# A hybrid decoder trunk on eight cores: the S5 scan and the dilated attention written in large operations, and TensorE's waits on its own semaphore left out

## The chip, the cores and the metric

The kernel runs on the eight cores of one Trainium2 chip. Each core runs the same program over one whole sequence of 8192 tokens (core c takes sequence c mod 4), in 32 tiles of 256 tokens. The metric is the device time of the slowest core in microseconds (us). The engines have their profile names here: PE is TensorE (matmuls) and PEld its weight loads, DVE is VectorE, ACT is ScalarE, POOL is GpSimd, and SP issues the DMAs. SBUF is the memory on the core from which the engines read, PSUM the banks into which matmuls sum, and an evacuation copies a bank to SBUF. In some executions the cores of one die (cores 0 to 3, or 4 to 7) show a lower granted clock and take longer; a run with one die over 1% longer than the other counts as slow.

## The reference

Two layers. Layer 0 has an SSD mixer and an S5 mixer side by side; layer 1 has causal attention in three patterns of (window, dilation), merged by their denominators. After each mixer comes a gated FFN. Norms, conditioning and the SSD mixer are left out here, because the change does not touch them.

```python
D_MODEL, BATCH, SEQ = 1024, 4, 8192
S5_N_GROUPS, S5_STATE = 64, 64                       # 4096 complex states
ATT_PATTERNS = ((128, 1), (512, 4), (2048, 16))      # (window, dilation); 8 heads of 128
FFN_HIDDEN = 2816

def complex_linear_combine(e1, e2):                  # h(t) = a * h(t-1) + b(t), complex
    a1r, a1i, b1r, b1i = e1
    a2r, a2i, b2r, b2i = e2
    return (a2r * a1r - a2i * a1i, a2r * a1i + a2i * a1r,
            a2r * b1r - a2i * b1i + b2r, a2r * b1i + a2i * b1r + b2i)
...
    bu_re = jnp.einsum('lgc,gpc->lgp', us, bb_re)    # S5: input, scan, output
    bu_im = jnp.einsum('lgc,gpc->lgp', us, bb_im)
    _, _, h_re, h_im = lax.associative_scan(complex_linear_combine, (ar, ai, bu_re, bu_im), axis=0)
    return jnp.einsum('lgp,gcp->lgc', h_re, c_re) - jnp.einsum('lgp,gcp->lgc', h_im, c_im)
...
def dilated_window_attention(q, k, v, window, dilation):
    # query t attends t - j*dilation, j = 0..window//dilation
    ...
    p = jnp.exp(s - s_max)
    den = jnp.sum(p, axis=-1, keepdims=True)
    o = jnp.einsum('brnhqk,brnkhe->brnqhe', p / den, vb)
...
def swiglu(h, w_in, w_out):
    g, u = jnp.split(h @ w_in, 2, axis=-1)
    return (jax.nn.silu(g) * u) @ w_out
```

## The kernel before

A small scheduler in Python records every operation with the buffers that it reads and writes, and derives the waits. A buffer keeps the token (engine, count) of its last writer. The engine that comes next waits for that count, even if it is itself the writer.

```python
    def _collect(self, eng, reads, writes, extra=()):
        waits = {}
        seen = self.seen[eng]

        def add(tok):
            if tok is None:
                return
            k, v = tok
            if seen.get(k, 0) >= v:
                return
            if waits.get(k, 0) < v:
                waits[k] = v

        for b in reads:
            add(b.w)
        for b in writes:
            add(b.w)
            for t in b.r:
                add(t)
        ...
```

So eight matmuls that sum into one PSUM bank each wait for the one before. Weights stream from DRAM in panels of up to 1 MB through three slots; a projection asks for a panel when it begins with it, and one DMA queue (SP) carries all loads and stores in program order.

```python
    def wpanel(self, name, kc, c0, cols, k0=0):
        slot = self.wp_rr
        self.wp_rr = (self.wp_rr + 1) % self.NW                  # NW = 3
        ...
        s.dma(lambda e, a=view, b=src: e.dma_start(out=a, in_=b), reads=[self.w_buf[name]], writes=[self.b_wp[slot]])
...
    def ffn(self, li):
        for mp in range(0, FC, 4):                               # FC = 22: six pairs of panels
            wg, bwg = self.wpanel(win, KC, mp * 128, nm * 128)
            wu, bwu = self.wpanel(win, KC, FFN_H + mp * 128, nm * 128)
            for mi in range(nm):
                # 8 matmuls with wg into one bank, 8 with wu into another, then silu and product
...
    def mixer1(self, ti):
        self.proj("attn_w_qkv", 0, 3072, KC, hrhs, self.b_h, on_q)
        def mk_kv(dst, bdst):
            def on_kv(mi, mw, ps, bps):
                q = mi % 2
                self.evac("act" if mi % 2 == 0 else "dve", self.kvst[:, q, :], ps[:, 0:NT], [bps], [self.b_kvst[q]])
                s.dma(lambda e: e.dma_start(out=dst[mi, :, 2048 + t0:2048 + t0 + NT], in_=self.kvst[:, q, :]),
                      reads=[self.b_kvst[q]], writes=[bdst])
            return on_kv
        self.proj("attn_w_qkv", 3072, 1024, KC, hrhs, self.b_h, mk_kv(self.Kd, self.b_Kd))
        self.proj("attn_w_qkv", 4096, 1024, KC, hrhs, self.b_h, mk_kv(self.Vd, self.b_Vd))
        for h in range(8):
            self.attn_head(ti, h)
```

The S5 mixer goes through blocks of 32 tokens, eight a tile. TensorE computes the inputs, ScalarE brings them to SBUF, VectorE (one half of the states) and GpSimd (the other) step through time, and TensorE forms the outputs. Attention goes key block by key block, up to 44 a head.

The softmax here doesn't subtract the row's maximum and nothing guards it: scores larger than these inputs give would overflow.

Of the kernel before, what the change touches and what calls it, by code (L numbers as in the profile page):

```python
# [24 lines left out]
class Sched:  # L25
# [22 lines left out]
    def _collect(self, eng, reads, writes, extra=()):  # L48
        waits = {}
        seen = self.seen[eng]  # L50

        def add(tok):
            if tok is None:
                return
            k, v = tok
            if seen.get(k, 0) >= v:
                return
            if waits.get(k, 0) < v:
# [8 lines that stand above are left out]
        for t in extra:  # L67
            add(t)
        for k, v in waits.items():
            seen[k] = v  # L70
        return list(waits.items())
# [14 lines left out]
    def op(self, eng, fn, reads=(), writes=()):  # L86
        waits = self._collect(eng, reads, writes)
# [103 lines left out]
class Builder:  # L191
# [18 lines left out]
    def _tensors(self):  # L210
# [46 lines left out]
        self.ps_rr = 0  # L257

    POOL_BANKS = (0, 1, 2, 3, 7)
# [173 lines left out]
    def _tensors_mix(self):  # L433
# [37 lines left out]
        self.Hall = self.sb("Hall", [128, 2, 32, 33], F32); self.b_Hall = [s.buf("Hall0"), s.buf("Hall1")]  # L471
        self.Hs16 = self.sb("Hs16", [128, 2, 32, 32], BF16); self.b_Hs16 = s.buf("Hs16")
        self.t12 = self.sb("t12", [128, 2, 2, 2, 16], F32); self.b_t12 = [s.buf("t12a"), s.buf("t12b")]
# [7 lines left out]
        assert o <= 7424, o  # L481
        a16 = self.A16
# [43 lines left out]
    def setup_mix(self):  # L526
# [15 lines left out]
        for hf in range(2):  # L542
            s.op("pool", lambda e, hf=hf: e.memset(self.Hall[:, :, hf * 16:(hf + 1) * 16, :], 0.0), writes=[self.b_Hall[hf]])
# [7 lines left out]
    def setup_s5(self):  # L551
# [12 lines left out]
        def coeffs(lr, li, ld, N, base):  # L564
# [3 lines left out]
            act(lambda e: e.activation(out=dt, in_=ld, func=AF.Exp))  # L568
            dve(lambda e: e.tensor_tensor(mag, lr, dt, ALU.mult))
# [27 lines left out]
        dve(lambda e, ai=ai: e.tensor_scalar(self.s5c[:, 3, :], ai, -1.0, None, ALU.mult), writes=[self.b_s5w])  # L597
        N = 128
# [147 lines left out]
    def ssd_chunk(self, c, ac, dtv, dtw, bd, idf):  # L746
# [11 lines left out]
        px, bpx = self.psum()  # L758
# [9 lines left out]
        pb, bpb = self.psum()  # L768
# [58 lines left out]
    def s5_sub(self, ts, T):  # L827
        s = self.s
        for b in range(4):
            ri = b // 2  # L830
            pb, bpb = self.psum()
            for slot in range(16):
                q = (b % 2) * 16 + slot
                fc, rb = q // 4, q % 4
                s.op("pe", lambda e, pb=pb, slot=slot, fc=fc, rb=rb, ri=ri: e.matmul(  # L835
                    pb[:, slot * T:(slot + 1) * T], self.Wb[32 * rb:32 * rb + 32, fc, ri, :], self.ubf[32 * rb:32 * rb + 32, fc, ts:ts + T],
                    start=True, stop=True, tile_position=(32 * rb, 0)), reads=[self.b_s5w, self.b_ubf[fc]], writes=[bpb])
            hf = b % 2
            s.op("act", lambda e, pb=pb, ri=ri, hf=hf: e.activation(out=self.Hall[:, ri, hf * 16:(hf + 1) * 16, 1:1 + T],  # L839
                                                                  in_=pb[:, :].rearrange("p (q t) -> p q t", q=16), func=AF.Copy),  # L840
                 reads=[bpb], writes=[self.b_Hall[hf]])
        for hf, eng in ((0, "dve"), (1, "pool")):
            qs = slice(hf * 16, (hf + 1) * 16)
            t1 = self.t12[:, hf, 0, :, :]
            t2 = self.t12[:, hf, 1, :, :]
            bh = self.b_Hall[hf]
            bt = self.b_t12[hf]
            for t in range(1, T + 1):
                s.op(eng, lambda e, t=t, t1=t1, qs=qs: e.tensor_tensor(t1, self.s5c[:, 0:2, qs], self.Hall[:, :, qs, t - 1], ALU.mult),  # L849
                     reads=[bh, self.b_s5w], writes=[bt])  # L850
                s.op(eng, lambda e, t=t, t2=t2, qs=qs: e.tensor_tensor(t2[:, 0, :], self.s5c[:, 3, qs], self.Hall[:, 1, qs, t - 1], ALU.mult),  # L851
                     reads=[bh, self.b_s5w], writes=[bt])
                s.op(eng, lambda e, t=t, t2=t2, qs=qs: e.tensor_tensor(t2[:, 1, :], self.s5c[:, 2, qs], self.Hall[:, 0, qs, t - 1], ALU.mult),  # L853
                     reads=[bh, self.b_s5w], writes=[bt])
                s.op(eng, lambda e, t1=t1, t2=t2: e.tensor_tensor(t1, t1, t2, ALU.add), reads=[bt], writes=[bt])  # L855
                s.op(eng, lambda e, t=t, t1=t1, qs=qs: e.tensor_tensor(self.Hall[:, :, qs, t], self.Hall[:, :, qs, t], t1, ALU.add),  # L856
                     reads=[bt], writes=[bh])
        s.op("act", lambda e: e.activation(out=self.Hs16[:, :, :, :], in_=self.Hall[:, :, :, 1:1 + T], func=AF.Copy),  # L858
             reads=self.b_Hall, writes=[self.b_Hs16])
        for hf, eng in ((0, "dve"), (1, "pool")):  # L860
            qs = slice(hf * 16, (hf + 1) * 16)
            s.op(eng, lambda e, qs=qs: e.tensor_copy(self.Hall[:, :, qs, 0], self.Hall[:, :, qs, T]), reads=[self.b_Hs16], writes=[self.b_Hall[hf]])
        po, bpo = self.psum()
        for fc in range(8):
            n = 0
            for rb in range(4):
                q = 4 * fc + rb
                for ri in range(2):
                    s.op("pe", lambda e, fc=fc, q=q, ri=ri, n=n: e.matmul(po[:, fc * T:(fc + 1) * T], self.Wc[:, q, ri, :], self.Hs16[:, ri, q, :],  # L869
                                                                         start=(n == 0), stop=(n == 7)),  # L870
                         reads=[self.b_s5w, self.b_Hs16], writes=[bpo])
# [4 lines left out]
    def s5_tile(self):  # L876
        s = self.s
        fv = self.fvec
        T = 32
# [44 lines left out]
    def attn_block(self, qap, nq, keys, ocols, Ob, bO, Db, bD):  # L924
        s = self.s
        scale = float(128 ** -0.5)
        n = len(keys)
        for i, (kap, nk, vidx, vbuf, mask) in enumerate(keys):
            pS, bpS = self.psum()
            slot = self.pt_rr  # L930
            self.pt_rr = (self.pt_rr + 1) % 4
            pt = self.PT[0:nk, slot, 0:nq]
            bpt = self.b_PT[slot]
            s.op("pe", lambda e, pS=pS, kap=kap, nk=nk: e.matmul(pS[0:nk, 0:nq], kap, qap, start=True, stop=True),  # L934
                 reads=[self.b_Kw] + self._qbufs, writes=[bpS])
            s.op("act", lambda e, pS=pS, pt=pt, nk=nk: e.activation(out=pt, in_=pS[0:nk, 0:nq], func=AF.Exp, scale=scale),  # L936
                 reads=[bpS], writes=[bpt])
            eng = "dve" if (slot % 2 == 0) else "pool"
            s.op(eng, lambda e, pt=pt, mask=mask: e.tensor_tensor(pt, pt, mask, ALU.mult), reads=[self.b_const], writes=[bpt])  # L939
            s.op("pe", lambda e, pt=pt, i=i, nk=nk: e.matmul(Db[:, ocols], self.ones_bf[0:nk, :], pt, start=(i == 0), stop=(i == n - 1)),  # L940
                 reads=[bpt, self.b_const], writes=[bD])
            s.op("pe", lambda e, pt=pt, i=i, vidx=vidx, nk=nk: e.matmul(Ob[:, ocols], self.Vtok[0:nk, vidx, :], pt, start=(i == 0), stop=(i == n - 1)),
                 reads=[bpt, vbuf], writes=[bO])
# [200 lines left out]
```

## Time and profile before

The median was 90664.84 us over the 13 runs (90652.80 to 90679.29). A stage is cut here from its first matmul to the first matmul of the next one, on the slowest core; the medians over the tiles are:

| stage | times a tile | us each | us a tile |
|---|---|---|---|
| S5 scan | 1 | 872 | 872 |
| attention | 1 | 689 | 689 |
| FFN, first half | 2 | 171 | 342 |
| QKV projection | 1 | 183 | 183 |
| FFN, second half | 2 | 89 | 178 |
| input projection with convolution | 1 | 146 | 146 |
| SSD | 1 | 127 | 127 |
| norms | 5 | 11 to 25 | 110 |
| gate and output projections | 1 | 95 | 95 |
| attention output projection | 1 | 31 | 31 |
| sum | | | 2773 |

Thirty-two tiles of 2.77 ms and a start-up of 2.03 ms make the 90.7 ms. (The prediction took one middle tile, of 2776 us.) Read such a table before the busy shares: no engine is above 42% here, and what a change is worth depends on which wait ends last in each stage. The lines themselves are in the prediction.

### The profile page before, as it was taken

The numbers are of one execution on the slowest core, as the hardware profiler recorded it, in microseconds if no ns is written. First come the engines' busy times: TensorE is split into PE (matmuls) and PEld (weight loads), VectorE is DVE, ScalarE is ACT, GpSimd is POOL, SyncE is SP. The second block draws the span as 40 slices with busy tenths as digits, with TensorE's granted clock in tenths as the row PEclk, the third lists the DMA queues.
The fourth block names the chain that finished last, engine by engine and source line by source line (L and its number), as shares of the span: only waits on it lengthen the run. The fifth ranks groups of instructions, "written<-read, shape, count | busy, mean of one in ns | idle before, by whom it ended". The sixth has DMA issues, their size and how long they took to land.

```text
span 90666.2 us, 767533 instructions; the slowest of 8 cores (90564.3 to 90666.2 us)
## 1 busy us (share of the span) xinstructions
PE 38409.4 (42%) x145736; PEld 16029.3 (18%) x145736; DVE 16584.6 (18%) x60884; ACT 8491.3 (9%) x23945; POOL 14519.8 (16%) x52112
## 2 busy tenths in 40 slices
PE   2434344344444443443434444434434344344344
PEld 1111111111111111111111111111111111111111
DVE  0122211122111222112221112211122211112111
ACT  0000010000010000100000100001000001000010
POOL 0111111111111111111111111111111111111111
DMA  3001011010010000110000100001101011000010
GB/s 115 27 23 29 20 32 33 20 29 24 27 33 26 24 28 21 33 32 21 28 22 28 33 24 26 27 22 33 31 21 30 21 30 33 22 28 26 23 33 28
DMA packets 3581367, 2648.37 MB, mean 29 GB/s; under 512 B 1541280, under 2 KB 3467424, under 8 KB 3569952
## 3 DMA queue, kind: packets, MB, share of 16 engines
q1 hardware_dynamic: 3577136, 2599.25, 9.7%
q8 instruction: 1765, 28.92, 0.1%
q14 instruction: 2466, 20.20, 0.1%
HBM read 2462.64 MB, written 136.35 MB: 29 GB/s over the span
## 4 chain that ended last, share of the span: by engine, by line
PE 43%; issue 28%; POOL 15%; ACT 5%; DVE 4%; DMA 3%; POOLq 1%; ACTq 0%; DVEq 0%; SPq 0%
PE ps L650 10%; PE ps L428 5%; PE ps L417 5%; PE ps L414 4%; PE ps L869 4%; PE ps L970 3%; PE ps L835 3%; POOL Hall L856 3%; POOL t L849 3%; PE ps L940 2%; POOL t L855 2%; ACT A L936 2%; POOL t L853 2%; POOL t L851 2%; PE ps L934 2%
## 5 line engine op out<-in xcount | busy, mean ns | idle before, releaser
L869 PE MATMUL ps<-Hs,Wc 128*128 128x32 bf16 x16384 | 3015.4, 184 | 19664.9 <-ACT Hs L858 17256.6
L650 PE MATMUL ps<-ht,wp 128*128 128x256 bf16 x17664 | 6253.0, 375 | 3240.5 <-DMA wp<-attn_w_qkv_bf 644.6
L940 PE MATMUL ps<-A,ones_bf 128*128 128x16 bf16 (+3 forms) x11096 | 2272.2, 205 | 10878.3 <-POOL A L939 5461.9
L939 POOL TENSOR_TENSOR A<-A,cmask_sb 16x16 bf16<-16x16 bf16 (+2 forms) x5548 | 1354.5, 244 | 26459.5 <-ACT A L936 26459.5
L869 PEld LDWEIGHTS ps<-Hs,Wc 128*128 128x128 bf16 x16384 | 1735.4, 106 | 20945.4 <-issue 20945.4
L414 PE MATMUL ps<-ht,wp 128*128 128x256 bf16 x11264 | 4223.4, 375 | 1761.0 <-ACT ht L384 313.7
L417 PE MATMUL ps<-ht,wp 128*128 128x256 bf16 x11264 | 4225.5, 375 | 1469.2
L428 PE MATMUL ps<-A,wp 128*128 128x256 bf16 x11264 | 4114.9, 372 | 1602.3
L970 PE MATMUL ps<-ident_bf,A 128*128 128x128 bf16 (+2 forms) x11008 | 2976.2, 282 | 2708.2 <-DMA A<-Vd 1294.8
L849 POOL TENSOR_TENSOR t<-s5c,Hall 128x32 f32<-128x32 f32 x8192 | 2267.9, 277 | 11393.3 <-ACT Hall L839 10236.8
L366 POOL TENSOR_TENSOR sq<-yt 128x256 bf16<-128x256 f32 x512 | 313.5, 612 | 22007.2 <-ACT yt L429 11833.3
L835 PE MATMUL ps<-A,Wb 32*128 32x32 bf16 x16384 | 2838.2, 181 | 2292.4 <-PE ps L835 107.8
L939 DVE TENSOR_TENSOR A<-A,cmask_sb 128x16 bf16<-128x16 bf16 (+3 forms) x5548 | 1080.6, 195 | 14581.4 <-ACT A L936 14580.8
L849 DVE TENSOR_TENSOR t<-s5c,Hall 128x32 f32<-128x32 f32 x8192 | 1936.1, 236 | 9468.8 <-ACT Hall L839 8614.2
L650 PE MATMUL ps<-A,wp 128*128 128x256 bf16 x8192 | 2931.5, 374 | 1213.6 <-ACT A L886 107.0
L936 ACT ACTIVATE A<-ps 128x16 bf16<-128x16 f32 (+3 forms) x11096 | 2162.4, 195 | 13163.4 <-PE ps L934 13152.9
L940 PEld LDWEIGHTS ps<-A,ones_bf 128*128 128x128 bf16 (+1 forms) x11096 | 1128.2, 102 | 11843.6 <-issue 11843.6
L650 PEld LDWEIGHTS ps<-ht,wp 128*128 128x128 bf16 x17664 | 1849.2, 105 | 7644.3 <-issue 7577.4
L374 DVE RECIPROCAL rstd<-rstd 128x256 f32<-128x256 f32 x320 | 560.9, 1753 | 10685.0 <-ACT rstd L371 10685.0
L369 PE MATMUL ps<-sq,ones_bf 128*128 128x256 bf16 x2304 | 854.7, 371 | 3876.9 <-POOL sq L366 1917.3
L934 PE MATMUL ps<-A 128*128 128x16 bf16 (+3 forms) x11096 | 2473.7, 223 | 15.2
L856 POOL TENSOR_TENSOR Hall<-Hall,t 128x32 f32<-128x32 f32 x8192 | 2278.2, 278 | 1193.4 <-POOL t L855 28.5
(174 smaller groups left out, 43787.5 us busy)
## 6 DMA issues: line engine op xcount, KB each, us to landing
wp<-ffn_w_in_bf SPq DMA_DIRECT2D x640, 1024.0 KB, 5.3
wp<-ffn_w_out_bf SPq DMA_DIRECT2D x512, 704.0 KB, 5.1
wp<-attn_w_qkv_bf SPq DMA_DIRECT2D x320, 1024.0 KB, 5.1
wp<-hyb_w_in_bf SPq DMA_DIRECT2D x224, 1024.0 KB, 5.3
A<-Kd SPq DMA_DIRECT2D x256, 576.0 KB, 4.0
A<-Vd SPq DMA_DIRECT2D x256, 576.0 KB, 5.0
wp<-hyb_w_out_bf SPq DMA_DIRECT2D x128, 1024.0 KB, 5.4
wp<-s_glu_w_bf SPq DMA_DIRECT2D x64, 1024.0 KB, 5.2
```

Of the source, the lines that this page charges most:

```text
L414: e.matmul(o, w, r, start=st, stop=sp), reads=[bwg, self.b_h[k]], writes=[bpg])
L417: e.matmul(o, w, r, start=st, stop=sp), reads=[bwu, self.b_h[k]], writes=[bpu])
L428: e.matmul(o, w_, r, start=st, stop=sp), reads=[bw, self.b_act[k]], writes=[bpo])
L650: e.matmul(o, w_, r, start=st, stop=sp), reads=[bw, rhs_bufs[k]], writes=[bps])
L835: s.op("pe", lambda e, pb=pb, slot=slot, fc=fc, rb=rb, ri=ri: e.matmul(pb[:, slot * T:(slot + 1) * T], self.Wb[32 * rb:32 * rb + 32, fc, r ...
L849: s.op(eng, lambda e, t=t, t1=t1, qs=qs: e.tensor_tensor(t1, self.s5c[:, 0:2, qs], self.Hall[:, :, qs, t - 1], ALU.mult), reads=[bh, self. ...
L856: s.op(eng, lambda e, t=t, t1=t1, qs=qs: e.tensor_tensor(self.Hall[:, :, qs, t], self.Hall[:, :, qs, t], t1, ALU.add), reads=[bt], writes= ...
L869: s.op("pe", lambda e, fc=fc, q=q, ri=ri, n=n: e.matmul(po[:, fc * T:(fc + 1) * T], self.Wc[:, q, ri, :], self.Hs16[:, ri, q, :], start=(n ...
L934: s.op("pe", lambda e, pS=pS, kap=kap, nk=nk: e.matmul(pS[0:nk, 0:nq], kap, qap, start=True, stop=True), reads=[self.b_Kw] + self._qbufs, ...
L936: s.op("act", lambda e, pS=pS, pt=pt, nk=nk: e.activation(out=pt, in_=pS[0:nk, 0:nq], func=AF.Exp, scale=scale), reads=[bpS], writes=[bpt])
L940: s.op("pe", lambda e, pt=pt, i=i, nk=nk: e.matmul(Db[:, ocols], self.ones_bf[0:nk, :], pt, start=(i == 0), stop=(i == n - 1)), reads=[bpt ...
L970: s.op("pe", lambda e, pvb=pvb, sl=sl, c0=c0, nk_=nk_: e.transpose(pvb[0:nk_, c0:c0 + 128], self.Vw[:, sl], self.ident_bf[:, :]), reads=[s ...
```

## The change

Its intent is to take the turns between engines, and TensorE's turns with itself, out of the path. It has four parts: TensorE no longer waits for its own earlier matmuls; the S5 scan becomes eleven large operations on VectorE, with tables of powers of the decay that are built once; an attention pattern becomes one round per head; and the PSUM banks are divided between matmuls and transposes.

```diff
-    def _collect(self, eng, reads, writes, extra=()):
+    def _collect(self, eng, reads, writes, extra=(), selfwait=True):
...
             k, v = tok
+            if eng == "pe" and k == "pe" and not selfwait:
+                return
...
-    def op(self, eng, fn, reads=(), writes=()):
-        waits = self._collect(eng, reads, writes)
+    def op(self, eng, fn, reads=(), writes=(), selfwait=False):
+        waits = self._collect(eng, reads, writes, selfwait=selfwait)
...
-    POOL_BANKS = (0, 1, 2, 3, 7)
+    POOL_BANKS = (0, 1, 2)
+    BF_BANKS = (3, 7)                       # transposes
...
+        for t in range(1, self.TS + 1):     # at start-up: decay^t and decay^-t, 64 sets
+            for tab, sgn in ((self.Tfwd, 1.0), (self.Tinv, -1.0)):
+                ar_t, ai_t = coeffs(..., ts=sgn * t)
...
     def s5_sub(self, ts, T):
-        for hf, eng in ((0, "dve"), (1, "pool")):
-            for t in range(1, T + 1):
-                # five operations of 16 or 32 elements: Hall[t] += decay * Hall[t-1]
-        s.op("act", ... Hs16 <- Hall ...)
+        # H holds the inputs, m is scratch; Br and Bi are H's real and imaginary parts
+        s.op("dve", ... tensor_tensor(m[:, 0:2], H, Tinv, mult))                 # 2048 elements
+        s.op("dve", ... tensor_tensor(m[:, 2], Br, Tinv[:, 1], mult))            # 1024, as the next three
+        s.op("dve", ... tensor_tensor(Bi, Bi, Tinv[:, 0], mult))
+        s.op("dve", ... tensor_tensor(Br, m[:, 0], m[:, 1], subtract))
+        s.op("dve", ... tensor_tensor(Bi, Bi, m[:, 2], add))
+        s.op("dve", ... tensor_tensor_scan(flat, smask, flat, 0.0, mult, add))   # running sum, 64 x 33
+        # the same four products and two sums with Tfwd, into Hs16 (bf16)
+        # two operations of 32 elements: the carry into column 0 of H
...
-    def attn_block(self, qap, nq, keys, ocols, Ob, bO, Db, bD):
-        for i, (kap, nk, vidx, vbuf, mask) in enumerate(keys):
-            # score matmul, exp, mask product, denominator matmul, output matmul
+    def attn_pat(self, ti, h, d, qoff, ...):
+        for r in range(d):
+            # score of the previous keys (128), then of the current keys (ncur), all into one bank
+        exp_mask(pS, bpS, parts)            # two exp, two mask products of 256 columns
+        # two denominator matmuls of 256 columns
+        for r in range(d):
+            # output matmul of the previous keys, then of the current keys
```

## The prediction

The prediction's 133 ns for a matmul of 256 columns without a wait is an estimate; the trace of the kernel before has 0.22 us for such a matmul. Its rival A is a slow clock, with these matmuls spaced 0.21 us.

> **What bounds the kernel now.** I read the page first (shares, chain, costliest groups), then the groups with shapes kept apart, the waits, the stages of one middle tile as windows, and last the timeline of single instructions. The page says that no engine is full: TensorE 42%, VectorE 18%, GpSimd 16%, and the chain that ended last is mostly TensorE plus "issue", time in which nothing visible was waited for.
>
> ```profile
> PE 38409.4 (42%) x145736; PEld 16029.3 (18%) x145736; DVE 16584.6 (18%) x60884; ACT 8491.3 (9%) x23945; POOL 14519.8 (16%) x52112
> ...
> PE 43%; issue 28%; POOL 15%; ACT 5%; DVE 4%; DMA 3%; POOLq 1%; ACTq 0%; DVEq 0%; SPq 0%
> ...
> L650 PE MATMUL ps<-ht,wp 128*128 128x256 bf16 x17408 | 6161.6, 375 | 3207.0 <-DMA wp<-attn_w_qkv_bf 644.6 <-ACT ht L384 312.2 <-PE ps L650 18.6
> ...
> L705 DVE TENSOR_TENSOR_SCAN dtt<-ones,dtt 16x128 f32<-16x128 f32 x64 | 26.4, 412 | 6.6
> ```
>
> The weight loads of one projection show where "issue" comes from (start, duration, then in brackets the idle time before).
>
> ```profile
> 40698.35 0.11 PEld L650 LDWEIGHTS ps<-ht,wp 128*128 128x128 bf16 x1 [0.41 <-issue]
> 40698.87 0.11 PEld L650 LDWEIGHTS ps<-ht,wp 128*128 128x128 bf16 x1 [0.41 <-issue]
> 40699.39 0.14 PEld L650 LDWEIGHTS ps<-ht,wp 128*128 128x128 bf16 x2 [0.41 <-issue]
> 40700.13 0.11 PEld L650 LDWEIGHTS ps<-ht,wp 128*128 128x128 bf16 x1 [0.60 <-issue]
> ```
>
> One load-and-matmul every 0.52 us: the scheduler counts the previous matmul as writer of the same bank, so each matmul waits for TensorE's own semaphore, with the array drained. The row "x2" is the exception: the first matmul of a new bank has no such wait, and the pair takes 0.74 us, so the unwaited one costs only 0.22.
>
> The stages of one tile of 2776 us (columns: window, length, busy time of the engines, clock, DMA share, GB/s), in this order: S5 scan, attention, input projection with convolution, first half and second half of the FFN, QKV.
>
> ```profile
> 46526.00:47398.00 872.00, 182.53 (x1025) 103.59 (x1024) 282.96 (x1295) 41.44 (x56) 331.79 (x1288) 1.00 0.00 1
> 47985.00:48673.00 688.00, 266.04 (x1398) 155.57 (x1398) 76.12 (x244) 94.64 (x393) 42.95 (x176) 1.00 0.05 17
> 46242.00:46388.00 146.00, 82.33 (x232) 24.14 (x232) 33.38 (x94) 22.51 (x42) 0.00 (x0) 1.00 0.19 57
> ...
> 47518.00:47688.00 170.00, 123.36 (x351) 36.93 (x351) 11.47 (x27) 13.58 (x31) 0.00 (x0) 1.00 0.19 57
> 47688.00:47777.00 89.00, 64.05 (x176) 18.54 (x175) 0.42 (x1) 2.69 (x7) 0.61 (x1) 1.00 0.32 76
> 47802.00:47985.00 183.00, 113.13 (x320) 33.66 (x320) 11.14 (x27) 11.91 (x28) 0.00 (x0) 1.00 0.16 53
> ```
>
> S5 and attention are 56% of a tile, and in both the engines take turns.
>
> ```profile
> PE ps L869 <- ACT Hs L858: 17256.6, 256, 68.2
> ACT Hs L858 <- POOL Hall L856: 16538.2, 256, 65.3
> ...
> DVE A L939 <- ACT A L936: 14580.8, 5296, 5.3
> ACT A L936 <- PE ps L934: 13152.9, 10578, 1.9
> ```
>
> In each of 256 S5 blocks TensorE waits about 68 us for a scan done in 32 steps of five tiny operations on VectorE and GpSimd; in attention every key block is one round score, exp, mask, sum.
>
> [...]the spacing of waited matmuls is 520 ns at 256 columns, 413 at 128 and 333 at 32, 0.83 ns a column[...], although the clock column says 1.00. [...]the built-in scan runs at half throughput; here 128 elements took 412 ns, what 256 take in a plain operation.
>
> **The change part by part**, per tile, from the stage lengths above.
>
> (1) TensorE's waits on itself go, everywhere. [...]I choose 133[...]. Then weights matter. A 1 MB panel lands 5.3 us after issue and streams in about 3.5 us; two back to back took 7.75. FFN first half: a chunk of 8 matmuls is P = 1.06 us; with three panel slots the next up-panel is issued only when the gate-panel is done, so a pair of panels takes 6P + 5.3 = 11.7 us, not 8P = 8.5. Six pairs (the last half as long): 8.5 + 4 x 11.7 + 6.3 = 62 us instead of 170. Second half: a 704 KB panel of 256-byte packets streams in 3.6 us alone and about 4.0 in a row, more than the 2.9 us of its 22 matmuls: 31 instead of 89. Both twice a tile: 2 x (108 + 58) = 332 us saved. QKV: 320 x 0.133 = 43 + 8 for keys and values through DRAM = 51 instead of 183 (132 saved). Input projection: 31 for the matmuls, then the 33 us of convolution that already follow them = 64 instead of 146 (82). Gate and output projections: 30 instead of 95 (65), attention output 10 instead of 31 (21). SSD keeps its chain over VectorE, ScalarE and GpSimd; only the transposes gain: 127 to 120 (7). The norms (95 us a tile in all) keep their chain of squares: nothing.
>
> (2) S5: the 160 small operations per block on each of two engines become eleven large ones on VectorE before the next matmul can start. [...]two of 2048 elements at 2.29 us, eight of 1024 at 1.22, one scan of 2112 at half rate, [...]4.56. Sum 4.6 + 9.8 + 4.6 = 18.9, and eleven gaps of 0.1 (the gap between dependent VectorE operations now): 20.1. Around it, in series because TensorE goes in order: 64 input matmuls without waits at 64 ns (my estimate for issuing two instructions of 31 ns, a spacing the trace shows), 4.1; four evacuations of 0.60 with gaps, 3.0; three hand-overs, 0.8; 64 output matmuls at about 0.1[...], 6.4. Together 34.4 us a block against 109; eight blocks and the entry 278 us instead of 872: 594 saved. GpSimd is idle here afterwards; it lost nothing by that.
>
> (3) Attention: 44 rounds a head become three. A round needs exp 0.38, mask 0.42, again 0.38 and 0.42 (one buffer, so in series) and hand-overs of 0.17: 2.7 us. TensorE around them: scores 0.5 + 1.6 + 4.2, denominators 3 x 0.43, outputs 0.4 + 0.9 + 3.4; rounds 3 x 2.7: 20.4 us. The 43 transposes go through two banks, and VectorE's first copy waits behind the previous head's additions and its 1.75 us reciprocal: 9 us. So 29 us a head, 232 for eight, against 688: 456 saved. The next head's keys are asked for some 6.5 us before the head ends and land in 5 to 5.5: just hidden.
>
> (4) Added: 64 coefficient sets at start-up, each about 25 tiny VectorE operations at 0.3, four ScalarE ones with hand-overs and two table loads of 1.28: 12.8 us, 0.82 ms in all. The conditioning matmuls at the start lose their wait: 0.2 ms back.
>
> Sum: 332 + 132 + 82 + 65 + 21 + 7 + 594 + 456 = 1689 us, 2776 - 1689 = 1087 us a tile. Times 32 = 34.8 ms, plus start-up 2.03 + 0.82 - 0.2 = 2.65: 37.4 ms.
>
> **The rivals.** A: [...]The 1856 wide matmuls a tile would cost 0.08 more each, less the stalls that they fill, about 120 us: 41 ms. B: DMA becomes the bound, eight cores drawing weights at 250 GB/s instead of 29. For: the panels above are already as long as their matmuls. Against: the bursts of today, 270 to 300 GB/s, come from cores that run the same program together. A fifth slower would cost some 70 us a tile: 39.7 ms. C: the drain wait was hidden behind other waits, so that (1) brings little, and S5 and attention alone shorten: 2776 - 1050 = 1726, 58 ms. The 0.22 against 0.52 in stages where TensorE sees no other wait speaks against it. D: S5's VectorE chain is shorter, with output matmuls at 0.06: 3 us a block less, 36.6 ms.
>
> **Range and chances.** The sum has hardly a term that could turn the sign. S5 (29 to 37 us a block) moves the total by 1.3 ms, attention (24 to 34 us a head) by 1.3, clock and DMA by 2 to 4, more upward. I predict 37500 us, 34000 to 42500. Faster by over 2%: 0.98; within 2%: 0.01; slower: 0.01.
>
> **What would show it.** Right: matmuls of 256 columns spaced 0.11 to 0.14 us, "issue" nearly gone from the chain; a scan of about 4.5 us and VectorE the longest part of a 34 us S5 block; waits on weight DMA in the FFN; two exp operations a round. Wrong: spacing at 0.21 (A), a granted clock far lower, 1 MB landings well above 5.3 us (B), or a VectorE operation of 2048 elements far from 2.29 us.

## The result, and the profile after

The changed kernel took 37037.93 us (median of 8 runs, 36898.68 to 37097.85). The ratio to the kernel before is 0.4083 (95% interval 0.4078 to 0.4087). All ratios here are the mean time of one kernel's fast runs over that of the kernel before in the same rounds, so they are not quite the ratio of the medians quoted. Executions in which one die ran at a lower clock are left out of the means. The result was correct.

The first fence is from the page of the changed kernel: the span, each engine's busy time with its share, the granted clock of TensorE in 40 slices, and the chain that ended last.

```profile
span 37052.1 us, 403605 instructions; the slowest of 8 cores (36874.4 to 37052.1 us)
...
PE 17304.2 (47%) x136176; PEld 12623.4 (34%) x136176; DVE 12397.6 (33%) x20575; ACT 6682.9 (18%) x14497; POOL 2549.4 (7%) x5350
...
PEclk9986656656666666565556556656655655665565
...
PE 38%; DVE 22%; DMA 14%; issue 11%; ACT 9%; POOL 3%; DVEq 1%; SPq 1%; ACTq 0%; POOLq 0%
```

"Issue" fell from 28% of 90.7 ms to 11% of 37.1 ms, that is from 25 ms to 4. DMA, 3% of the chain before, is now 14%, or 5 ms. The page before had no clock row, and its clock column read 1.000 for every core; now most slices read 5 or 6. That is not a loss: the traces of the kernel before and of e1 hold no clock entry at all, and the spacing of the matmuls shows that the array was slower then. Before, the spacing of waited matmuls (333 ns at 32 columns, 413 at 128, 520 at 256) grew by 0.83 ns a column; now most matmuls of 256 columns (72% on the slowest core) follow each other in 0.109 or 0.131 us, 0.43 or 0.51 ns a column (below).

The next fence shows one tile by stages, in the order of the prediction's windows (S5, attention, input projection, FFN first half, FFN second half, QKV), with the same columns.

```profile
18811.50:19027.20 215.70, 30.20 (x1025) 28.56 (x1024) 153.40 (x112) 26.50 (x48) 0.00 (x0) 0.50 0.00 1
18205.20:18450.50 245.30, 164.99 (x1097) 117.42 (x1098) 65.01 (x116) 45.12 (x89) 0.00 (x0) 0.51 0.14 47
18615.90:18683.80 67.90, 33.81 (x232) 25.28 (x233) 33.33 (x93) 21.89 (x42) 0.00 (x0) 0.64 0.42 126
18485.90:18561.60 75.70, 56.31 (x352) 41.57 (x353) 11.38 (x27) 13.35 (x30) 0.00 (x0) 0.71 0.42 122
18561.60:18588.70 27.10, 23.97 (x179) 18.69 (x176) 0.42 (x1) 2.70 (x7) 0.61 (x1) 0.81 0.98 186
18121.20:18205.20 84.00, 51.52 (x321) 38.12 (x322) 10.97 (x26) 11.31 (x27) 0.00 (x0) 0.65 0.35 115
```

In S5, VectorE is busy 153 of 216 us: the stage now has a bounding engine. In the second half of the FFN the DMA share is 0.98, so that stage is bound by its weights. In QKV and the first half of the FFN neither TensorE nor the DMA is full: they wait for one another. The medians over all tiles, beside what was predicted:

| stage | before | predicted | after |
|---|---|---|---|
| S5 scan | 872 | 278 | 216 |
| attention | 689 | 232 | 245 |
| FFN first half (each of two) | 171 | 62 | 75 |
| FFN second half (each of two) | 89 | 31 | 28 |
| QKV | 183 | 51 | 84 |
| input projection | 146 | 64 | 68 |
| gate and output projections | 95 | 30 | 27 |
| attention output projection | 31 | 10 | 12 |
| SSD | 127 | 120 | 117 |
| norms, together | 110 | unchanged | 103 |
| tile (predicted from 2776) | 2773 | 1087 | 1078 |
| start-up (ms) | 2.03 | 2.65 | 2.51 |

The total is nearly exact because errors of opposite sign met: S5 came out 62 us shorter, QKV 33, the FFN's first halves together 26 and attention 13 us longer.

**S5.** VectorE's timeline of one block (start, duration, line, operation; in brackets the idle time before and what ended it):

```profile
18871.86 2.29 DVE L871 TENSOR_TENSOR A<-Hall,Tinv 128x2048 f32<-128x2048 f32 x1 [7.23 <-ACT Hall L868]
18874.26 1.22 DVE L873 TENSOR_TENSOR A<-Hall,Tinv 128x1024 f32<-128x1024 f32 x1
18875.40 1.22 DVE L875 TENSOR_TENSOR Hall<-Hall,Tinv 128x1024 f32<-128x1024 f32 x1
...
18878.99 4.56 DVE L879 TENSOR_TENSOR_SCAN Hall<-smask,Hall 128x2112 f32<-128x2112 bf16 x1
...
18889.27 1.22 DVE L888 TENSOR_TENSOR Hs<-A,Hall 128x1024 bf16<-128x1024 f32 x1
```

The durations 2.29, 1.22 and 4.56 are those predicted, to the hundredth. The gaps are not: the second operation starts 0.11 us after the end of the first, but the third starts 1.14 us after the second's start, before its recorded end. From the first start to the last end it is 18.6 us. VectorE then waits about 7.2 us, while TensorE forms outputs and the next inputs:

```profile
18890.63 1.84 PE L900 MATMUL ps<-Hs,Wc 128*128 128x32 bf16 x63 [0.95 <-DVE Hall L890]
18892.41 1.86 PE L863 MATMUL ps<-A,Wb 32*128 32x32 bf16 x64
```

Sixty-three output matmuls of 32 columns, each with weights of its own, are over in 1.84 us, a spacing of 0.027.

**QKV.** TensorE's timeline:

```profile
18124.84 30.21 PE L674 MATMUL ps<-ht,wp 128*128 128x256 bf16 x218 [0.35 <-ACT ht L393]
18163.99 6.32 PE L674 MATMUL ps<-ht,wp 128*128 128x256 bf16 x32 [8.95 <-DMA wp<-attn_w_qkv_bf]
18177.40 6.41 PE L674 MATMUL ps<-ht,wp 128*128 128x256 bf16 x32 [7.08 <-DMA wp<-attn_w_qkv_bf]
18190.85 6.49 PE L674 MATMUL ps<-ht,wp 128*128 128x256 bf16 x32 [7.05 <-DMA wp<-attn_w_qkv_bf]
```

The seven panels of queries and the first keys stream without a break; before each of the last three panels TensorE stands for 7 to 9 us, and the 32 matmuls after it take 6.4 us (0.2 each, at a granted clock of 0.56 in the first of the three) where the stream before had 0.139 (at 0.78). The DMA queue's own timeline in that stretch says why:

```profile
18152.52 5.97 SPq L942 DMA_DIRECT2D Kd<-A  x4
18158.64 0.37 SPq L362 DMA_DIRECT2D wp<-attn_w_qkv_bf  x1
```

The four stores of keys of one panel stand in the queue before the load of the next panel. A store waits for its evacuated matmuls, so the load is asked for only when the panel before has been computed and stored.

**FFN, first half.** A part of the chain that ended last (start, duration, engine, what):

```profile
18496.81 1.06 PE ps L423 x8
18497.95 5.33 DMA wp<-ffn_w_in_bf
18503.53 1.82 PE ps L426 x8
18505.35 1.71 PE ps L423 x8
18507.06 1.09 PE ps L426 x8
```

The stall that the prediction expected is there: the panel begins when the gate panel is done, and lands 5.33 us later. What it did not expect are the next two lines: the first two groups of eight matmuls after the stall take 1.7 to 1.8 us to the next instead of 1.05. The granted clock is 0.51 in these two groups and 0.80 in the groups after them.

**The spacing of wide matmuls.** The intervals between successive matmuls of 256 columns over the whole trace of the slowest core, core 5, lie at three values: 0.109 us (36% of them), 0.131 (36%) and 0.213 (17%); the other 11% lie between these or are longer. The clock entries of this trace fit them: nearly all intervals of 0.109 lie where the granted clock is 1.00, of 0.131 where it is 0.81, and of 0.213 where it is 0.50. The dies differ, although both run the same program on the same four sequences: on cores 0 to 3 about 71% are 0.109 and only 1% are 0.131, on cores 4 to 7 28 to 36% are 0.131. Before, the usual interval was 0.520.

### The profile page after: what moved, and what is told of

It is laid out like the page before. It is cut to its first block, busy times and chain, and to the rows that moved or that the text cites.

```text
span 37052.1 us, 403605 instructions; the slowest of 8 cores (36874.4 to 37052.1 us)
## 1 busy us (share of the span) xinstructions
PE 17304.2 (47%) x136176; PEld 12623.4 (34%) x136176; DVE 12397.6 (33%) x20575; ACT 6682.9 (18%) x14497; POOL 2549.4 (7%) x5350
## 4 chain that ended last, share of the span: by engine, by line
PE 38%; DVE 22%; DMA 14%; issue 11%; ACT 9%; POOL 3%; DVEq 1%; SPq 1%; ACTq 0%; POOLq 0%
PE ps L674 8%; DMA wp<-ffn_w_in_bf 5%; PE ps L426 4%; PE ps L423 3%; DVE Hall L879 3%; DMA wp<-ffn_w_out_bf 3%; PE ps L970 2%; PE ps L437 2%; PE ps L1021 2%; PE ps L987 2%; PE ps L989 2%; PE ps L972 2%; PE ps L819 2%; DVE A L1035 2%; ACT Hall L868 2%
## 5 line engine op out<-in xcount | busy, mean ns | idle before, releaser
L900 PE MATMUL ps<-Hs,Wc 128*128 128x32 bf16 x16384 | 519.7, 188 | 5817.4 <-DVE Hs L886 5574.1
L674 PE MATMUL ps<-ht,wp 128*128 128x256 bf16 x17664 | 2600.8, 317 | 1173.0 <-DMA wp<-attn_w_qkv_bf 783.3
L674 PEld LDWEIGHTS ps<-ht,wp 128*128 128x128 bf16 x17664 | 1960.6, 112 | 1816.0 <-issue 1368.0
L426 PE MATMUL ps<-ht,wp 128*128 128x256 bf16 x11264 | 1928.4, 329 | 1245.2 <-DMA wp<-ffn_w_in_bf 1245.2
L900 PEld LDWEIGHTS ps<-Hs,Wc 128*128 128x128 bf16 x16384 | 479.1, 104 | 5858.8 <-issue 5858.4
L658 ACT ACTIVATE A<-ps 128x256 bf16<-128x256 f32 (+4 forms) x2176 | 1187.5, 558 | 5817.8 <-PE ps L1021 3220.0
L423 PE MATMUL ps<-ht,wp 128*128 128x256 bf16 x11264 | 1949.4, 321 | 349.3 <-ACT ht L393 318.0
L426 PEld LDWEIGHTS ps<-ht,wp 128*128 128x128 bf16 x11264 | 1288.3, 116 | 1666.5 <-issue 1331.8
L1021 PE MATMUL ps<-ident_bf,A 128*128 128x128 bf16 (+2 forms) x11008 | 1364.6, 307 | 982.5 <-DVE A L660 610.1
L437 PE MATMUL ps<-A,wp 128*128 128x256 bf16 x11264 | 1501.4, 298 | 329.0 <-DMA wp<-ffn_w_out_bf 289.0
L423 PEld LDWEIGHTS ps<-ht,wp 128*128 128x128 bf16 x11264 | 1284.3, 114 | 800.2 <-issue 491.4
L1021 PEld LDWEIGHTS ps<-ident_bf,A 128*128 128x128 bf16 (+2 forms) x11008 | 1081.3, 147 | 1222.1 <-issue 1213.8
L437 PEld LDWEIGHTS ps<-A,wp 128*128 128x128 bf16 x11264 | 1168.0, 106 | 658.2 <-issue 443.2
L674 PE MATMUL ps<-A,wp 128*128 128x256 bf16 x8192 | 1161.1, 308 | 229.9 <-ACT A L917 148.2
L970 PE MATMUL ps<-A 128*128 128x16 bf16 (+1 forms) x4960 | 1198.2, 242 | 0.0
```

What stands on the lines that cost most here:

```text
L423: e.matmul(o, w, r, start=st, stop=sp), reads=[bwg, self.b_h[k]], writes=[bpg])
L426: e.matmul(o, w, r, start=st, stop=sp), reads=[bwu, self.b_h[k]], writes=[bpu])
L437: e.matmul(o, w_, r, start=st, stop=sp), reads=[bw, self.b_act[k]], writes=[bpo])
L658: s.op("act", lambda e: e.activation(out=out, in_=in_, func=AF.Copy), reads=reads, writes=writes)
L674: e.matmul(o, w_, r, start=st, stop=sp), reads=[bw, rhs_bufs[k]], writes=[bps])
L900: s.op("pe", lambda e, fc=fc, q=q, ri=ri, n=n: e.matmul(po[:, fc * T:(fc + 1) * T], self.Wc[:, q, ri, :], self.Hs16[:, ri, q, :], start=(n ...
```

## The experiments

Diffs are against the changed kernel unless another is named. They ran in several rounds and on several chips; the kernel before took 90624 to 90691 us (medians) in these rounds, and the changed kernel's own runs spread over 0.2 ms.

### e1: the waits back, the rest of the change kept

```diff
-    def op(self, eng, fn, reads=(), writes=(), selfwait=False):
+    def op(self, eng, fn, reads=(), writes=(), selfwait=True):
```

> The changed kernel with TensorE's waits on itself put back, so the new S5 scan and the new attention alone. Theory (the two halves of the change are nearly independent; the new S5 and attention still gain, but pay 0.33 to 0.42 us a matmul): an S5 block is 21 + 3 + 19 + 21 = 64 us against 109 before, a head about 59 us against 86, every other stage as before; a tile 2776 - 352 - 213 = 2211 us, in all about 73 ms. Rival 1 (S5 and attention carry nearly the whole gain, the waits were hidden): below 60 ms. Rival 2 (the rewrites only pay together with the waits gone): above 82 ms.

It took 69169 us (2 runs, ratio 0.763). The stages in which nothing else was changed went back to their old lengths: FFN first half 170, QKV 183, input projection 146. S5 took 410, where some 520 had been expected, and attention 454. The S5 miss has its reason in TensorE's timeline:

```profile
40428.09 8.56 PE L863 MATMUL ps<-A,Wb 32*128 32x32 bf16 x64
```

These 64 input matmuls go round four banks, so that a wait is for the matmul four back: 0.13 us each, not the 0.33 that a wait for the last one costs. The clock column reads 1.000 on all cores again.

### e2: the waits alone, on the kernel before

The four row tiles of the old S5 input share a bank, so that they keep their wait.

```diff
 (against the kernel before)
+            if eng == "pe" and k == "pe" and not selfwait:
+                return
...
-    def op(self, eng, fn, reads=(), writes=()):
+    def op(self, eng, fn, reads=(), writes=(), selfwait=False):
...
-                    ... tile_position=(32 * rb, 0)), reads=[...], writes=[bpb])
+                    ... tile_position=(32 * rb, 0)), reads=[...], writes=[bpb], selfwait=True)
```

> The kernel before, with TensorE's waits on itself removed and nothing else (kept only on the S5 input matmuls, whose row tiles share a bank). Theory: FFN, projections and QKV fall to what they are in the changed kernel; S5 loses only the waits of its 64 output matmuls, 872 to about 720 us; attention loses only those of its transposes, 688 to about 585, because its rounds of score, exp, mask, sum stay; a tile about 1920 us, in all 63 ms. Rival C of the prediction (the drain wait was hidden behind other waits): above 80 ms.

It took 61301 us (2 runs, ratio 0.676); FFN 76 and 28, QKV 84, S5 720, attention 524 (some 585 expected, a miss), start-up 1.81 ms. Rival C, that the drain wait was hidden anyway, falls. The rewrite alone saves 90.7 - 69.2 = 21.5 ms, the waits alone 29.4 ms, both 53.6 ms, 2.7 ms more than the sum. The surplus is in the two rewritten stages: taking the waits away saves 152 + 165 us a tile there in the old form (872 to 720, 689 to 524), but 194 + 209 in the new one (410 to 216, 454 to 245), and 32 x 86 us are 2.75 ms. In S5 this needs no interplay of the two halves: e2 kept the waits of the old input matmuls, while e1 against the changed kernel counts the input matmuls too (8.56 us a block in e1, 1.86 after), and 8 x 6.7 = 54 us cover the 42. The 44 us in attention were not taken apart. The start-up splits likewise: the tables cost 2.51 - 1.81 = 0.70 ms, and the waits had cost 0.2.

### e3: QKV panels asked for two ahead

```diff
-        for p0 in range(0, ncols, pc):
+        for n_, p0 in enumerate(starts):
-            w, bw = self.wpanel(wname, nk, c0 + p0, pw, k0=k0)
+            while len(loaded) < len(starts) and len(loaded) <= n_ + ahead:
+                loaded.append(self.wpanel(...))
+            w, bw = loaded[n_]
...
-        three projections: 3072, 1024 and 1024 columns
+        self.proj("attn_w_qkv", 0, 5120, KC, hrhs, self.b_h, on_qkv, ahead=2)
```

> The changed kernel with the QKV weight panels asked for two panels ahead, so that no store of keys or values stands before a load in the one DMA queue. Theory (QKV took 84 us and not 51 because each of the last three loads is queued behind the stores of the panel before[...]): the waits of 9.0, 7.1 and 7.0 us[...] go, QKV 84 to about 56 us, 32 x 28 us = 0.9 ms, 36.1 ms, ratio 0.975 to the changed kernel. Rival (the loads are slow because stores and loads share the DMA engines' bandwidth): QKV stays above 75 us, within 1% of the changed kernel.

It took 36575 us (4 runs, ratio 0.403), and QKV 67 us instead of the 56 expected: half a miss. The DMA queue shows what was left:

```profile
18085.99 7.37 SPq L946 DMA_DIRECT2D Kd<-A  x4
18093.51 0.37 SPq L362 DMA_DIRECT2D wp<-attn_w_qkv_bf  x1
18094.63 8.74 SPq L946 DMA_DIRECT2D Kd<-A  x4
```

Four stores now take 7 to 9 us, more than the panel's matmuls. By the code, all heads' keys are one buffer to the scheduler, so each store waits until the one before has landed; and there are two staging tiles, so that the evacuation, and then TensorE, wait for the stores. The next run takes both away at once.

### e10: the same, with a buffer for each head and eight staging tiles

```diff
 (against e3)
-        self.b_Kd = s.buf("Kd"); self.b_Vd = s.buf("Vd")
+        self.b_Kd = [s.buf("Kd%d" % h) for h in range(8)]; self.b_Vd = [...]
-                q = mi % 2
-                self.evac(..., self.kvst[:, q, :], ps[:, 0:NT], [bps], [self.b_kvst[q]])
+                q = mi
+                self.evac(..., self.attn[:, q, :], ps[:, 0:NT], [bps], [self.b_attn[q]])
```

> The QKV run once more (panels two ahead), with the stores of keys and values freed too: each head has its own write order, so a store no longer waits until the one before has landed, and eight staging tiles take the place of two, so an evacuation does not wait for a store that stands behind a 1 MB load. Theory (this is what kept QKV at 67 us in the first form and not at 56): 50 us, as in the run of all together; 32 x 34 us below the changed kernel's 84, 36.0 ms, ratio 0.971 to the changed kernel. Rival (QKV gains in the run of all together came from the other changes): 60 us or more.

It took 35970 us (4 runs, ratio 0.397), and QKV 49.5 us: as expected. The same group of four stores:

```profile
18730.53 2.98 SPq L946 DMA_DIRECT2D Kd<-A  x4
```

In this profile all eight cores stream at 0.109, as do cores 0 to 3 of the changed kernel, where QKV takes 80 to 82 us. So about 31 of the 34 us a tile between 83.6 and 49.5 are shown to be the order of the queue and the waits of the stores in it, with the slow matmuls that follow each wait; some 3 us are the faster spacing.

### e4: a fourth slot for the FFN's panels

The slot lies in a region that only attention uses.

```diff
-        slot = self.wp_rr
-        self.wp_rr = (self.wp_rr + 1) % self.NW
+        slot = self.wp_rr if self.wp_rr < nslots else 0
+        self.wp_rr = (slot + 1) % nslots
+        flat = self.A16[:, 13312:13312 + kc * cols] if slot == 3 else self.wp[:, slot, 0:kc * cols]
...
-            wg, bwg = self.wpanel(win, KC, mp * 128, nm * 128)
+            wg, bwg = self.wpanel(win, KC, mp * 128, nm * 128, nslots=4)
```

> The changed kernel with a fourth weight slot in the FFN (in a part of the arena that is idle then). Theory (the first half is held by the third slot: the up-panel is asked for only when the gate-panel is done[...]): stalls go, the spacing stays at 0.131, the first half goes from 75 to about 53 us, 64 x 22 us = 1.4 ms, 35.6 ms, ratio 0.962. Rival (eight cores together are at the limit of what memory gives): waits on the panels remain, first half above 68 us.

It took 35273 us (4 runs, ratio 0.389), and the first half 49 us (53 expected). After three slow groups at its start, TensorE's timeline of one tile's first half has one wait for weights, of 0.98 us, and no slow group any more:

```profile
18311.12 1.04 PE L427 MATMUL ps<-ht,A 128*128 128x256 bf16 x8
18311.99 1.04 PE L424 MATMUL ps<-ht,wp 128*128 128x256 bf16 x8
```

Groups of eight follow each other in 0.87 us, 0.109 a matmul. Over the whole kernel the share of the 0.213 spacing falls from 17% to 9%, and in the FFN's first half from 6080 of 22528 intervals to 1040, nearly all of these in its first 8 us. So the slow matmuls after a stall vanish with it, and those at the start of the stage stay (three groups of eight, 1.4 to 1.7 us apart).

### e5 and e11: a second state buffer for S5, so that the next inputs lie beside VectorE's chain

Both give the state a second buffer and move the next block's input matmuls and evacuations ahead of the output matmuls; they differ in where the code stands, and so in what the scheduler sees.

```diff
+        Hn = self.Hal2[1 - i]                # the next block's buffer
+        if ts + T < NT:                      # e11: here, ahead of the DVE operations
+            self.s5_in(ts + T, T, 1 - i)
         ... the DVE operations ...
-        s.op("dve", ... H[:, 0, :, 0] <- carry ...)
+        s.op("dve", ... Hn[:, 0, :, 0] <- carry ...)
+        if ts + T < NT:                      # e5: here, after the carry
+            self.s5_in(ts + T, T, 1 - i)
```

> The changed kernel with a second state buffer in S5: the input matmuls and evacuations of the next block are issued before the output matmuls of this one, so only VectorE's chain is left in series. Theory (a block of 26.2 us is 18.6 of VectorE and 7.6 of TensorE, ScalarE and hand-overs in series with it): a block falls to 19.1 to 19.6 us, S5 from 215.7 to about 163 us, 32 x 52 us = 1.7 ms, 35.4 ms, ratio 0.955 to the changed kernel. Rival (ScalarE writing the next state slows VectorE, or the tables' reads are the limit): the VectorE operations get longer than 1.22 and 2.29 us and the block stays above 23 us.

It took 36065 us (4 runs, ratio 0.398): a block 21.9 us, not 19.3. A miss. VectorE's timeline shows the carry, then the first operation of the next block:

```profile
18576.55 0.21 DVE L903 TENSOR_TENSOR Hall<-A 128x32 f32<-128x32 f32 x1
18579.73 2.29 DVE L882 TENSOR_TENSOR A<-Hall,Tinv 128x2048 f32<-128x2048 f32 x1 [2.97 <-ACT Hall L870]
```

The carry writes column 0 of the next buffer, and the evacuation writes its other columns. To the scheduler that is one buffer, so that the evacuation, which comes later in the program, waited for the carry.

> The second state buffer once more, with the next block's input matmuls and evacuations issued before VectorE's chain of this block, not after it. In the first form the evacuation waited for the last two small VectorE operations, which write column 0 of the same buffer. Theory: VectorE's chain is then the only thing in series, a block falls from 21.85 to 18.9 to 19.5 us, S5 to about 160 us, 35.3 ms. Rival (the 3 us between blocks are hand-overs that stay): 21 us or more a block, 36.0 ms.

It took 35480 us (4 runs, ratio 0.391), a block 19.0 us, as expected; the same two lines:

```profile
19276.03 0.21 DVE L905 TENSOR_TENSOR Hall<-A 128x32 f32<-128x32 f32 x1
19276.35 2.29 DVE L884 TENSOR_TENSOR A<-Hall,Tinv 128x2048 f32<-128x2048 f32 x1
```

VectorE is now without a pause, and 19.0 us is its eleven operations and the carry. That confirms both terms of the S5 sum: 18.6 us of VectorE and 7.6 us of other work in series with it.

### e7: attention's matmuls grouped by shape

In the changed kernel a matmul on 128 old keys alternates with one on 64 or 16 current keys. Here all of one shape come first. The outputs of a bank become one accumulation group.

```diff
-        for r in range(d):
-            if has_prev: score of previous keys r
-            score of current keys r
+        for r in range(d if has_prev else 0): score of previous keys r
+        for r in range(d): score of current keys r
 (the outputs likewise, with start only on the first and stop only on the last)
```

> The changed kernel with the score and output matmuls of the two dilated patterns grouped by shape: all of the 128-key blocks first, then all of the short ones, the same matmuls otherwise. They now alternate between full and partial shapes, spaced 0.172 and 0.137 us, while S5's equal ones of 32 columns are spaced 0.027. Theory[...]: the spacing falls below 0.11, a head loses 4 to 6 us of 30.9, attention 245 to about 205 us, 1.3 ms, 35.7 ms. Rival (the strided weights or the small size set the spacing): it stays near 0.15 and the time within 1%.

It took 35139 us (4 runs, ratio 0.388), and attention 182 us (205 expected, 245 before). First the changed kernel, then e7:

```profile
18314.96 0.24 PE L970 MATMUL ps<-A 128*128 128x16 bf16 x1
18315.12 0.20 PE L972 MATMUL ps<-A 128*16 128x16 bf16 x1
```

```profile
18480.23 1.19 PE L970 MATMUL ps<-A 128*128 128x16 bf16 x16
...
18485.17 0.61 PE L987 MATMUL ps<-A 128*128 128x16 bf16 x16
```

(The first column of sizes is the array, here 128*128 or 128*16.) Alternating, starts are 0.14 to 0.17 us apart; in a group of one shape sixteen scores take 1.19 us (0.063 apart) and sixteen outputs 0.61 (0.027 apart). The number of matmuls is the same. The single accumulation group is no rival for the scores, which have none and gain as well. Why the scores of one shape are not as fast as the outputs was not tested.

### e9: the matmul inputs after each pre-norm set to zero (a wrong result)

```diff
+                for z in range(2):
+                    s.op("dve", lambda e, out=self.vec[:, li, half * 3 + z, :]: e.memset(out, 0.0), ...)
```

> The changed kernel with the norms' scale and shift set to zero, so that the moving data of the dense matmuls is zero (a wrong result on purpose). Theory[...]: the spacing of the 256-column matmuls falls to 0.109 in FFN and QKV; the time hardly moves, 36.3 to 37.0 ms, because the panels' landings bind there. Rival (0.131 is how fast weights and data can be read or issued): it stays at 0.131.

The run asks whether the spacing of 0.131 depends on the data. One look: 36910 us, relative error 0.53. On the slowest core the spacing of 0.131 has all but vanished (0.3% of the intervals), 0.109 has risen to 71%, and 0.213 is where it was (18%). In the changed kernel the two spacings go with the clock: 0.109 / 0.131 is 0.83, and the granted clock is 1.00 at the one and 0.81 at the other. e9's trace has no clock entry of 0.81 on any core, while every profiled run with real data and without the waits has at least five on each. But the run does not show that the data are the cause of the fall from 36%. Cores 0 to 3 of the changed kernel itself, with real data, stand at about 1%, and in e10 all eight cores are under 2%. Here is a group of eight matmuls of one line in two cores that work on the same sequence (core 1, then core 5), both from the profile of the changed kernel:

```profile
18498.89 1.04 PE L426 MATMUL ps<-ht,wp 128*128 128x256 bf16 x8
18509.02 1.23 PE L426 MATMUL ps<-ht,wp 128*128 128x256 bf16 x8
```

What decides between the two stays open; several runs of e9 would be needed. The time hardly moved: 36910 lies inside the changed kernel's own range. The first half of the FFN takes 75 us as before, with groups of eight at 0.87 us, for the panels hold it: they land in 6.0 to 6.4 us in the median of a core, against 5.9 to 6.2 in the changed kernel.

### e8 and e12: all together

e8 is e4, e7, e10 and e5 in one kernel; e12 has e11's order in place of e5's.

```diff
 (e12 against e8)
+        if ts + T < NT:
+            self.s5_in(ts + T, T, 1 - i)     # ahead of the DVE operations
...
-        if ts + T < NT:
-            self.s5_in(ts + T, T, 1 - i)     # after the carry
```

> All together: four weight slots in the FFN, QKV panels ahead (and, since that run showed stores of keys and values serialised and queued, one write order for each head and eight staging tiles in place of two), the second S5 state buffer, the grouped attention matmuls. Theory (the waits are in different stages and add up): 1.8 + 1.0 + 1.7 + 1.3 ms less than 37.0, 31.3 ms. Rival (the weight DMA binds once the rest is gone): above 33 ms.

It took 31393 us (4 runs, ratio 0.347), with QKV 50, FFN first half 48, attention 183.

> All improvements together with the S5 order of the run above. Theory: 7 x 2.5 us a tile less than the first version of all together (31.4 ms), 30.8 ms. Rival: no change, 31.4 ms.

It took 30640 us (4 runs, 30528 to 30722, ratio 0.338), correct: 17% under the changed kernel and the fastest. The four savings by themselves were 1.77 (e4), 1.90 (e7), 1.07 (e10) and 1.56 ms (e11), 6.29 in all; together they are 6.40. So they touch four separate waits, as the stage table says; the difference is within the spread of the runs. Its page:

```profile
PE 34%; DVE 27%; issue 13%; DMA 10%; ACT 10%; POOL 4%; SPq 1%; DVEq 1%; ACTq 0%; POOLq 0%
```

VectorE's part of the chain has risen to 27%: S5 now is a pure VectorE stage.

### e13: two of S5's products on the idle GpSimd

```diff
 (against e12)
-        s.op("dve", lambda e: e.tensor_tensor(m[:, 2, :, :], Br, self.Tinv[:, 1, :, :], ALU.mult),
+        s.op("pool", lambda e: e.tensor_tensor(m[:, 2, :, :], Br, self.Tinv[:, 1, :, :], ALU.mult),
 (and the same product with Tfwd)
```

> As the run above, but two of the eleven VectorE operations of an S5 block (the products that make the third temporary) go to GpSimd, which is idle. Theory (independent engines): VectorE's chain loses 2 x 1.14 us a block, 0.55 ms in all, 30.3 ms. Rival (the two engines get in each other's way[...], and GpSimd needs some 3 us for 1024 elements): the VectorE operations beside it get longer than 1.22 and 2.29 us and the time stays or grows.

It took 31099 us (3 fast runs, ratio 0.343; the slow one took 31304), half a millisecond slower than e12. One of the pairs, from the timelines of VectorE and GpSimd:

```profile
18859.28 3.00 DVE L904 TENSOR_TENSOR Hall<-Hall,Tfwd 128x1024 f32<-128x1024 f32 x1
```

```profile
18856.99 4.21 POOL L902 TENSOR_TENSOR A<-Hall,Tfwd 128x1024 f32<-128x1024 f32 x1 [7.33 <-DVE Hall L898]
```

The product takes GpSimd 3.1 to 4.2 us, and VectorE's operation beside it 3.00 instead of 1.22. In the other pair VectorE's operation keeps 1.2 us, but GpSimd's product takes 3.1 us instead of the 2.2 of its shortest, and VectorE then stands 2.1 us for it. Why the two slow each other was not tested. GpSimd idle was not GpSimd free to use here.

## Why the prediction was right

The time, the range and the direction held; the steps one by one:

- **(1) The waits go, everywhere.** Right, and shown by e1 and e2 from both sides. The period of 133 ns was an estimate; it stands for a mixture of 109, 131 and 213 on core 5, and almost only of 109 and 213 on cores 0 to 3. FFN second half 28 against 31, gate and output 27 against 30, attention output 12 against 10, SSD 117 against 120: all near. The input projection, 68 against 64, is 4 us over.
- **FFN first half, "6P + 5.3 = 11.7".** The mechanism is right (e4 removes it), and its size is off: a pair takes 13.5 to 13.8. Two groups after each stall run at a granted clock of 0.50 to 0.51 instead of 0.80 to 0.81 and cost 0.65 us more each, and the stall is 3.6 to 4.0 us instead of 3.2, as a panel's landing has a median of 5.9 us.
- **QKV, "320 x 0.133 = 43 + 8".** This step failed. It took the matmuls and the keys' way through DRAM, but no wait for weights, although the quoted line of before shows 644.6 us on "DMA wp<-attn_w_qkv_bf", 20 us a tile, which no removed wait touches. The 84 us are 3.6 at the start, where the norm's output is still being written, 30.2 of stream, 23.1 of three waits, 19.2 for the last 96 matmuls (12.8 was predicted) and 7.9 for keys and values (8 was predicted). e10 takes the three waits and the slow matmuls away together, and the stage is 49.5. So the step was missing a term and not mistaken in those that it had, apart from the last 96 matmuls.
- **(2) S5, 34.4 us a block.** It is 26.2. The durations were exact, and agree with the trace before: there a plain operation takes 424 ns for 256 elements and 1219 for 1024, that is 1.04 ns for one element more and 2.28 us for 2048, and a scan of 128 elements takes 412 ns, as a plain operation of 256 on as many partitions. Three terms were mis-sized: the output matmuls (6.4 predicted, 1.8 measured), the input matmuls (4.1 against 1.9), and "eleven gaps of 0.1" (VectorE takes 18.6 us from first start to last end, where 20.1 was predicted). The evacuations and hand-overs took 3.9 where 3.8 was predicted. The 0.1 us for an output matmul was an estimate from the recorded duration of a weight load, 0.106. After, the loads are recorded at 0.104, and yet a load with its matmul follows the one before in 0.027.
- **(3) Attention, 29 us a head.** 30.9, near. The alternation of shapes, which e7 shows to cost 245 - 182 = 62 us a tile, was not seen as a term of its own; it hid in the TensorE sums, which come to 12.3 us a head in the prediction and to about 16 in the timeline. The rounds (2.2 to 2.6 us instead of 2.7) and the transposes took less than predicted, so that the total came near with the help of opposite errors.
- **(4) Tables.** 0.82 ms predicted, 0.70 measured (after against e2); the 0.2 ms of waits at the start was right.
- **The norms: nothing.** They gained 7 us a tile, small but not nothing. (They are 110 us by the table's cut, not 95.)
- **Rivals.** A (slow clock) is partly true: 17% of the matmuls are spaced 0.213, at a granted clock of 0.50, in the FFN after stalls and at the start of a stage and not all over, as e4 shows. B (DMA as a common bound) is not seen: the panels of 1 MB land in 5.3 to 7.4 us (medians by weight, 5.1 to 5.4 before, without the 10.6 of the attention output), and only the second half of the FFN, as predicted, is bound by its weights (DMA share 0.98). C falls by e2. D (a shorter S5) had the right direction, and S5 fell even further than D's 3 us a block.
- **The signs.** The spacing of 0.11 to 0.14, the scan of 4.56 us, the waits on weights in the FFN and two exp a round all came. "Issue nearly gone" did not: it is still 11% of the chain, 4 ms.

That the predicted 37500 us came within 1.3% owes something to luck: with S5 predicted at its true length, the sum of 37.4 ms would have been 35.4, which is 1.6 ms under the measured time.

## What to carry to other kernels

A wait of TensorE on itself cost 0.30 us at every matmul of 256 columns here (0.52 us, 0.22 for one without the wait before the change), and the array was slower all along as well (0.11 to 0.13 us once the waits were gone); no busy share shows it: look at the spacing of weight loads and at "issue" in the chain. When such waits go, whatever stood behind them in time becomes visible: in an in-order queue, a store that waits holds back the load behind it (TensorE stood 7 to 9 us before each of three panels in QKV), and a buffer that covers more than it must turns into a wait (2.97 us before a block in e5). A DMA wait that the old profile shows stays in the sum unless the change touches its cause (20 us a tile before, 23 after, in QKV); and place loads so that a stall never occurs, because TensorE paid for it twice here (3.6 to 4.0 us in the FFN's first half, and 1.3 us more in the two groups after it).
